# A quarter of an output projection between the steps of the last head pair

## The chip, the cores and the metric

The kernel runs on one core of a Trainium2 chip. The metric is the device time of one execution in microseconds (us); the time of a kernel is the median of its runs. Engines are named as in the profile: PE (TensorE, the matrix engine), PEld (its weight loads), DVE (VectorE), ACT (ScalarE), POOL (GpSimd) and SP (SyncE, which here issues nearly all DMA transfers, in order, on one queue). A name with q (SPq) is an engine's queue.

## The reference

One inference step of a two-layer encoder on 640 frames: 512 of a new stream (the prompt) and 16 each of 8 running streams (the samples). Layer 0 is a convolution module and a gated feed-forward network (FFN); layer 1 is attention over a shared K and V, and an FFN. Cut to the attention:

```python
k, v = jnp.split(rms_norm(h, norm_kv) @ w_kv, 2, axis=-1)
q = (rms_norm(h, norm_attn[j]) @ w_q[j]).reshape(B, T, N_HEADS, HEAD_DIM)
if past_k is None:                                   # the prompt
    o = band_attention_prompt(q, k, v, rel_bias[j])
else:                                                # the samples, with 512 cached rows
    o = band_attention_sample(q, jnp.concatenate([past_k, k], axis=1),
                              jnp.concatenate([past_v, v], axis=1), rel_bias[j])
h = h + o @ w_o[j]
h = h + swiglu(rms_norm(h, norm_ffn[l]) @ w_ffn_in[l]) @ w_ffn_out[l]
```

There are 16 heads of 64 and 1024 features. All data are float32.

## The kernel before

Features lie on the 128 partitions and frames along the free axis, so `h` is 8 feature tiles (KT = 8) of 640 columns (NT), the 128 sample frames first. Each operand of a large matmul is split into a high part (float32r) and a low part, and a product is three matmuls (`mm3`, lines 167 to 169). `wsplit` loads 2048 columns of weights and splits them (ACT the high part, line 147; DVE the low part, line 151), two buffers in turn; `xsplit` splits activations (lines 156 and 157).

The instructions of each engine run in the order in which the compile step puts them: a scheduler with a time model takes them by readiness and by the order in which the program issues them, and a `high_priority` block moves its instructions forward.

The attention goes through 8 head pairs `p` (two heads of 64 fill the 128 partitions). The steps of a pair stand in a string, BO for pairs 0 to 6 and BL for the last:

- `a0`, `a1` (`head_a`): the prompt's scores of one head (lines 1049 and 1050), the maxima with the bias added (DVE, line 959), exponentials (ACT, line 952) and scaling.
- `s0`, `s1` (`samp_a`): scores of four running streams each. Two tiles of cached keys and two of cached values are loaded (line 1100, 512 KB each, tag `cache`, CB = 5 buffers); the scores are lines 1105 and 1108. They go into the PSUM tile that the head of the same number left.
- `b0`, `b1` (`head_b`): transposes of the probabilities (line 1073).
- `t0`, `t1` (`samp_b`): the same for the samples (lines 1121 and 1123).
- `p0` (`pair_c`): probabilities times V for both heads (line 1090), and the split of the result into `oT[p]`.
- `c0`, `c1` (`samp_c`): probabilities times cached V (line 1136) and new V (line 1140), scaling, a transpose (line 1148) and the split.

Between two pairs the next pair's K and Q are projected (`proj_kq`) and, every second pair, V (`proj_v`). After pair 2 `proj_o(0)` adds the output projection of pairs 0 and 1 to `h`, after pair 4 `proj_o(1)` that of pairs 2 and 3. The rest, pairs 4 to 7, follows the loop: for each half of the columns (NH = 320) and each of 8 feature tiles one PSUM tile collects 12 matmuls (4 pairs, three each), and one DVE instruction adds it to `h` (line 1195). `mm` has two PSUM tiles for all of this.

Then the FFN begins. Its first normalisation needs all 8 feature tiles of the first column half: squares (ACT, line 175), sums (POOL or DVE, line 194; PE, line 203), the power (POOL, line 244), the spread over the partitions (PE, line 215), a copy (ACT, line 524), the products (DVE, line 528) and the splits (ACT, line 319; DVE, line 320). Its matmuls are line 383.

Of the kernel before, what the change touches and what calls it, by code (L numbers as in the profile page):

```python
# [12 lines left out]
ALU = mybir.AluOpType  # L13
# [38 lines left out]
NXA, NXB = NB * SEG + HIST + HA, HIST + 320  # L52
SSQ = 'avavavav'
SCUT = 8
CB, QB, KB = 5, 1, 1
NSTD = 3
NH = NT // 2
X11, X21, XT2, XT1, XT3, XT4, X22 = range(7)
# [1 line left out]
HIX = {X11: 0, X21: 1, XT1: 2, XT2: 3, XT3: 4, X22: 5, XT4: 6}  # L60
QORD = "50 a0 10 a1 20 51 11 60 30 21 70 61 31 40 52 71 12 22 41 62 32 53 72 13 23 42 63 33"
BO = "a0 s0 a1 s1 b0 b1 t0 p0 c0 t1 c1"
BL = "a0 s0 a1 s1 t0 b0 b1 c0 t1 c1 p0"
SSQ1 = 'ppapappp'
LNO = ((0, 1, 4, 5, 6, 2, 3, 7), (0, 1, 4, 2, 3, 5, 6, 7))
PLAN = ("a0 y x1 b0 b1 q0 dp1s0 c2 ds1p2 D3 C4 S3 q3 ds2 C5 E6 S4 A4 F6 B4 E7 S5 A5 F7 S6 A6 S7 "
# [8 lines left out]
def tile_trunk(ctx, tc, xT, vecs, hist, w_pw1, w_pw2, w_in0, w_out0, w_os0, w_in1, w_out1, w_os1,  # L75
# [884 lines left out]
                                       op0=ALU.add, op1=ALU.max, accum_out=mx)  # L960

    kts, qts, vts, oT = {}, {}, {}, {}

    def proj_kq(p):
        wh, wl = wsplit(w_kq[p], 16, P, gains=GKQ)
# [57 lines left out]
    def head_a(p, hh):  # L1023
        kt, qt = kts[p], qts[p]
        r = slice(hh * DH, hh * DH + DH)
        S = sp.tile([P, 1280], F32, tag="S", name=nm("S"))
        mx = ap.tile([P, 4], F32, tag="mx", name=nm("mx"), bufs=3)
        sm = ap.tile([P, 4], F32, tag="sm", name=nm("sm"), bufs=3)
        wide = w2t()
        st = w2t()  # L1030
        ro = slice(DH - hh * DH, 2 * DH - hh * DH)
        KK = ap.tile([P, 512], F32R, tag="KK", name=nm("KK"), bufs=KB)
        KL = ap.tile([P, 512], F32R, tag="KL", name=nm("KL"), bufs=KB)
        QQ = ap.tile([P, 512], F32R, tag="QQ", name=nm("QQ"), bufs=KB)
        nc.scalar.activation(out=KK[r], in_=kt[r, P:], func=AF.Copy)
        nc.scalar.activation(out=QQ[r], in_=qt[r, P:], func=AF.Copy)
        nc.gpsimd.tensor_copy(KK[ro], KK[r].bitcast(F32))
        for to in (r, ro):
            nc.vector.tensor_tensor(out=KL[to], in0=kt[r, P:], in1=KK[r].bitcast(F32),
                                    op=ALU.subtract)  # L1040
        nc.vector.tensor_tensor(out=QQ[ro], in0=qt[r, P:], in1=QQ[r].bitcast(F32),
                                op=ALU.subtract)
        pss = []
        for i in ORD:
            n = (i + 1) * P
            o = SOFF[i]
            q = slice(i * P, (i + 1) * P)
            ps = st[:, 640:896] if i == 1 else wide[:, o:o + n]
            nc.tensor.matmul(ps, QQ[:, q], KK[:, 0:n], start=True, stop=False)
            nc.tensor.matmul(ps, QQ[:, q], KL[:, 0:n], start=False, stop=True)  # L1050
            pss.append(ps)
        for ii, i in enumerate(ORD):
            n = (i + 1) * P
            o = SOFF[i]
            addmax(S[:, o:o + n], pss[ii], BP[:, hh, 512 - n:512], mx[:, ii:ii + 1])
        rs = softmax_rows(S, mx, sm, [(SOFF[i], (i + 1) * P) for i in ORD])
        for ii, i in enumerate(ORD):
            n = (i + 1) * P
            o = SOFF[i]
            nc.vector.tensor_scalar(out=S[:, o:o + n], in0=S[:, o:o + n],  # L1060
                                    scalar1=rs[:, ii:ii + 1], scalar2=None, op0=ALU.mult)
        return S, st

    def head_b(S):
        PT = sp.tile([P, 1280], F32, tag="PT", name=nm("PT"))
        for kk in ((0,), (1, 3), (2,)):
            tr = amt()
            base = POFF[kk[0]]
            tot = 0
            for k in kk:  # L1070
                for i in range(k, 4):
                    o = POFF[k] - base + (i - k) * P
                    nc.tensor.transpose(tr[:, o:o + P],  # L1073
                                        S[:, SOFF[i] + k * P:SOFF[i] + (k + 1) * P], ident)
                    tot += P
            if kk[0] == 0:
                nc.scalar.activation(out=PT[:, base:base + tot], in_=tr[:, :tot], func=AF.Copy)
            else:
                nc.vector.tensor_copy(PT[:, base:base + tot], tr[:, :tot])
        return PT  # L1080

    def pair_c(p, PTs):
        VT = vts[p // 2]
        po = amt()
        for k in range(4):
            n = (4 - k) * P
            for hh in range(2):
                r = slice(hh * DH, hh * DH + DH)
                v0 = (p % 2) * P + hh * DH
                nc.tensor.matmul(po[r, k * P:512], VT[:, 1 + k, v0:v0 + DH],  # L1090
                                 PTs[hh][:, POFF[k]:POFF[k] + n], start=(k == 0), stop=(k == 3))
        xsplit(po, oT[p][0][:, P:], oT[p][1][:, P:])

    def samp_a(p, u, st):
        qb, kt = qbd[p % 2], kts[p]
        cache = []
        for src in (kc[p, u], vc[p, u].rearrange("p b k d -> p b (k d)")):
            for i in range(2):
                t = ap.tile([P, 2, 512], F32, tag="cache", name=nm("cache"), bufs=CB)
                nc.sync.dma_start(t, src[:, 2 * i:2 * i + 2, :])  # L1100
                cache.append(t)
        KC, VC = cache[:2], cache[2:]
        qv = [qb[:, 4 * u + b, :, :].rearrange("p h q -> p (h q)") for b in range(4)]
        for b in range(4):
            nc.tensor.matmul(st[32 * b:32 * b + 32, 0:512], qv[b], KC[b // 2][:, b % 2, :],  # L1105
                             start=True, stop=True)
        for b in range(4):
            nc.tensor.matmul(st[32 * b:32 * b + 32, 512:576], qv[b], kt[:, 64 * u:64 * u + 64],
                             start=True, stop=True)
        S = ap.tile([P, 576], F32, tag="Ss", name=nm("Ss"), bufs=2)  # L1110
        mx = ap.tile([P, 4], F32, tag="mx", name=nm("mx"), bufs=3)
        sm = ap.tile([P, 4], F32, tag="sm", name=nm("sm"), bufs=3)
        addmax(S, st[:, 0:576], BS, mx[:, 0:1])
        rs = softmax_rows(S, mx, sm, [(0, 576)])
        return S, rs, VC

    def samp_b(u, S):
        v0 = 64 * u
        tr = amt()
        for k in range(4):  # L1120
            nc.tensor.transpose(tr[:, k * P:(k + 1) * P], S[:, k * P:(k + 1) * P], ident)
        tn = amt()
        nc.tensor.transpose(tn[0:v0 + 64, 0:P], S[:, 512 - v0:576], ident)
        PT = ap.tile([P, 640], F32, tag="PTs", name=nm("PTs"), bufs=1)
        nc.scalar.activation(out=PT[:, 0:512], in_=tr, func=AF.Copy)
        nc.vector.tensor_copy(PT[v0:v0 + 64, 512:640], tn[v0:v0 + 64, 0:P])
        return PT

    def samp_c(p, u, PT, rs, VC):
# [3 lines left out]
        for k in range(5):  # L1133
            for b in range(4):
                if k < 4:
                    nc.tensor.matmul(pv[32 * b:32 * b + 32, 0:P],  # L1136
                                     PT[:, k * P + 32 * b:k * P + 32 * b + 32],
                                     VC[b // 2][:, b % 2, k * P:(k + 1) * P], start=(k == 0), stop=False)
                else:
                    nc.tensor.matmul(pv[32 * b:32 * b + 32, 0:P],  # L1140
                                     PT[v0:v0 + 64, 512 + 32 * b:512 + 32 * b + 32],
                                     VT[v0:v0 + 64, 0, (p % 2) * P:(p % 2) * P + P],
                                     start=False, stop=True)
        os_ = ap.tile([P, P], F32, tag="os", name=nm("os"), bufs=1)
        nc.vector.tensor_scalar(out=os_, in0=pv[:, 0:P], scalar1=rs[:, 0:1], scalar2=None,
                                op0=ALU.mult)
# [3 lines left out]
        for hh in range(2):  # L1150
            r = slice(hh * DH, hh * DH + DH)
            xsplit(trv[r, :, hh, :],
                   oT[p][0][r, v0:v0 + 64].rearrange("p (b q) -> p b q", q=SB),
                   oT[p][1][r, v0:v0 + 64].rearrange("p (b q) -> p b q", q=SB))

    run(proj_kq(0), proj_v(0))
    for p in range(NP):
# [8 lines left out]
        for op in (BL if p == NP - 1 else BO).split():  # L1166
# [5 lines left out]
            elif op[0] == "b":  # L1172
                pt[i] = head_b(ha[i][0])
            elif op[0] == "t":
                ps[i] = samp_b(i, sa[i][0])
            elif op[0] == "c":
                samp_c(p, i, ps[i], *sa[i][1:])
            else:
                pair_c(p, (pt[0], pt[1]))
        if p + 1 < NP:  # L1180
# [3 lines left out]
        if p in PO:  # L1184
            proj_o(PO[p])

    wos = [wsplit(w_o[r], 16, P) for r in (2, 3)]
    for g0, n in ((0, NH), (NH, NH)):
        for m in range(KT):
            pt = mmt()  # L1190
            mm3(pt[:, :n], [(wh[:, (k * 8 + m) * P:(k * 8 + m + 1) * P],
                             wl[:, (k * 8 + m) * P:(k * 8 + m + 1) * P])
                            for wh, wl in wos for k in range(2)],
                [(oT[4 + k][0][:, g0:g0 + n], oT[4 + k][1][:, g0:g0 + n]) for k in range(4)])
            nc.vector.tensor_tensor(out=h[:, m, g0:g0 + n], in0=pt[:, :n], in1=h[:, m, g0:g0 + n],
                                    op=ALU.add)
    at.close()
    early.close()

# [118 lines left out]
```

## Time and profile before

| | |
|---|---|
| time, median of 3 runs | 1525.98 us (1524.56 to 1526.48) |
| the profiled execution | 1530.94 us, span 1528.9 us |
| PE, matmuls | 1456.1 us busy (95%) |
| DVE | 1120.0 us (73%) |
| ACT | 746.7 us (49%) |
| POOL | 281.8 us (18%) |
| DMA | 192.57 MB, 126 GB/s |

Busy times are of the one profiled execution. The span is the time between the first and the last instruction in the trace. A busy PE is not a PE at its peak: matmuls are pipelined, and at a lower granted clock the same matmul is longer. All times of a timeline are microseconds from the span's start. Rows of the view by stretches give start and end, the length, then the busy time of each engine with its instructions in brackets.

### The profile page before, as it was taken

To read this page: it belongs to the slowest core of one execution; us is meant where nothing else is said; L and a number is where in the kernel's file an instruction comes from. 1 tells how busy PE (TensorE), PEld (TensorE's weight loads), DVE (VectorE), ACT (ScalarE), POOL (GpSimd) and SP (SyncE) were. 2 spreads that over 40 slices of the span, in tenths; PEclk is the share of its full clock that TensorE was granted. 3 is DMA by queue.
4 is the path that set the end of the run, shared out by engine and by line. 5 is a ranking of instruction groups with operands and counts; after the bars stand their busy time and mean duration, and the time that the engine had idled before them with its cause. 6 is when DMAs were issued, how large, how long until landed. Compare 5 with 4: busy or idle time off the path is not lost.

```text
span 1528.9 us, 28150 instructions
## 1 busy us (share of the span) xinstructions
PE 1456.1 (95%) x10974; PEld 1378.4 (90%) x10974; DVE 1120.0 (73%) x2481; ACT 746.7 (49%) x1617; POOL 281.8 (18%) x312
## 2 busy tenths in 40 slices
PE   5999899999999999999999999988999999999995
PEld 5998689999999999999887888957999999999994
DVE  5789346798888887856676667653799788688844
ACT  3666245464554563545554454442465464464432
POOL 5789232000000000013221121011000001001001
PEclk9999889999999999999999999988999999999997
DMA  7267414134444444424555455551124543444501
GB/s 236 65 185 182 102 48 132 44 101 117 149 116 126 139 116 132 111 83 149 193 188 189 138 173 187 168 166 42 56 76 111 158 127 93 143 138 92 169 29 69
DMA packets 71013, 192.57 MB, mean 126 GB/s; under 512 B 12000, under 2 KB 33248, under 8 KB 62432
## 3 DMA queue, kind: packets, MB, share of 16 engines
q1 hardware_dynamic: 61664, 175.78, 35.7%
q0 software_dynamic: 8928, 14.68, 6.4%
q8 instruction: 86, 1.41, 0.4%
q10 hardware_dynamic: 288, 0.31, 0.1%
q14 instruction: 47, 0.39, 0.1%
HBM read 179.14 MB, written 11.61 MB: 125 GB/s over the span
## 4 chain that ended last, share of the span: by engine, by line
PE 77%; DVE 8%; POOL 5%; DMA 5%; ACT 3%; issue 2%; SPq 0%; POOLq 0%; DVEq 0%; ACTq 0%
PE mm L383 44%; PE mm L167 7%; PE mm L168 7%; PE mm L169 7%; POOL ca L730 4%; PE mm L768 2%; DMA raw<-in_w_in 1%; PE w L1105 1%; PE w L203 1%; PE am L1090 1%; DVE wlo L320 1%; DMA cache<-in_ck 1%; PE am L1073 1%; PE am L1136 1%; DMA s<-in_w_in 1%
## 5 line engine op out<-in xcount | busy, mean ns | idle before, releaser
L383 PE MATMUL mm<-XH,whi 128*128 128x320 f32 x896 | 275.8, 310 | 4.5 <-DVE t L397 3.0
L383 PE MATMUL mm<-XH,wlo 128*128 128x320 f32 x896 | 276.5, 310 | 0.0
L383 PE MATMUL mm<-XL,whi 128*128 128x320 f32 x896 | 273.8, 309 | 0.0
L319 ACT ACTIVATE whi<-raw 128x512 fp32r<-128x512 f32 (+2 forms) x280 | 166.3, 612 | 156.7 <-PE mm L383 90.5
L167 PE MATMUL mm<-xh,whi 128*128 128x320 f32 (+2 forms) x640 | 202.0, 317 | 4.6 <-ACT xh L156 2.6
L168 PE MATMUL mm<-xh,wlo 128*128 128x320 f32 (+2 forms) x640 | 201.2, 315 | 0.6 <-DVE wlo L151 0.6
L169 PE MATMUL mm<-xl,whi 128*128 128x320 f32 (+2 forms) x640 | 198.1, 314 | 0.0
L320 DVE TENSOR_TENSOR wlo<-raw,whi 128x512 fp32r<-128x512 f32 (+2 forms) x280 | 183.6, 670 | 14.1 <-ACT whi L319 12.7
L383 PE MATMUL mm<-hid,whi 128*128 128x320 f32 x732 | 172.2, 309 | 2.6 <-ACT whi L319 2.3
L383 PEld LDWEIGHTS mm<-XH,whi 128*128 128x128 f32 x896 | 167.8, 188 | 6.5 <-DVE t L397 3.5
L383 PEld LDWEIGHTS mm<-XH,wlo 128*128 128x128 f32 x896 | 168.2, 188 | 0.5 <-DVE wlo L320 0.5
L383 PEld LDWEIGHTS mm<-XL,whi 128*128 128x128 f32 x896 | 167.6, 188 | 0.0
L167 PEld LDWEIGHTS mm<-xh,whi 128*128 128x128 f32 x640 | 122.5, 192 | 8.1 <-ACT xh L156 3.1
L383 PEld LDWEIGHTS mm<-hid,whi 128*128 128x128 f32 x732 | 124.9, 188 | 4.0 <-ACT whi L319 3.4
L365 POOL DMA_DIRECT2D s<-in_w_in x38 | 33.8, 890 | 503.9 <-DVE XL L320 115.7
L168 PEld LDWEIGHTS mm<-xh,wlo 128*128 128x128 f32 x640 | 122.7, 192 | 1.2 <-DVE wlo L151 0.8
L169 PEld LDWEIGHTS mm<-xl,whi 128*128 128x128 f32 x640 | 121.5, 191 | 1.2 <-issue 1.0
L383 PE MATMUL mm<-hid,wlo 128*128 128x320 f32 x366 | 112.5, 308 | 0.0
L383 PE MATMUL mm<-XL,shi 128*128 128x320 f32 x344 | 105.4, 308 | 1.3 <-DVE XL L320 1.3
L383 PE MATMUL mm<-XH,shi 128*128 128x320 f32 x344 | 106.0, 308 | 0.4 <-ACT XH L319 0.4
L383 PE MATMUL mm<-XH,slo 128*128 128x320 f32 x344 | 106.0, 308 | 0.1
L319 ACT ACTIVATE shi<-raw 128x512 fp32r<-128x512 f32 (+1 forms) x114 | 66.4, 587 | 73.5 <-PE mm L383 38.6
(229 smaller groups left out, 3368.7 us busy)
## 6 DMA issues: line engine op xcount, KB each, us to landing
raw<-in_w_in SPq DMA_DIRECT2D x38, 1024.0 KB
raw<-in_w_os SPq DMA_DIRECT2D x24, 768.0 KB
cache<-in_ck SPq DMA_DIRECT2D x32, 512.0 KB
cache<-in_cv SPq DMA_DIRECT2D x32, 512.0 KB
raw<-in_w_pw SPq DMA_DIRECT2D x12, 1024.0 KB
s<-in_w_in SPq DMA_DIRECT2D x38, 256.0 KB
s<-in_w_in POOLq DMA_DIRECT2D x38, 256.0 KB, 4.8
raw<-in_w_kq SPq DMA_DIRECT2D x8, 1024.0 KB
```

Of the source, the lines that this page charges most:

```text
L167: nc.tensor.matmul(ps, wh, xh, start=(i == 0), stop=False)
L168: nc.tensor.matmul(ps, wl, xh, start=False, stop=False)
L169: nc.tensor.matmul(ps, wh, xl, start=False, stop=(i == last))
L203: nc.tensor.matmul(st[:, 512 + t * w + k:513 + t * w + k], s[:, a:a + P], onec, start=True, stop=True)
L319: nc.scalar.activation(out=hi, in_=src, func=AF.Copy)
L320: nc.vector.tensor_tensor(out=lo, in0=src, in1=hi.bitcast(F32), op=sub)
L365: nc.gpsimd.dma_start(s1, src[:, 3 * n:4 * n], accum_op=add)
L383: nc.tensor.matmul(pt, wt, v, start=(first and k == i == 0), stop=(k == len(xs) - 1 and i == 2), skip_group_check=True)
L730: nc.gpsimd.tensor_tensor(out=acc, in0=acc, in1=pr, op=ALU.add)
L768: nc.tensor.matmul(pt[32 * q:32 * q + 32, 0:n], w4[0:r, 4 * tg + q, :], mv, start=(tg == 0), stop=(tg == 7))
L1073: nc.tensor.transpose(tr[:, o:o + P], S[:, SOFF[i] + k * P:SOFF[i] + (k + 1) * P], ident)
L1090: nc.tensor.matmul(po[r, k * P:512], VT[:, 1 + k, v0:v0 + DH], PTs[hh][:, POFF[k]:POFF[k] + n], start=(k == 0), stop=(k == 3))
```

## The change

The output projection of pairs 4 and 5 (weights `w_o[2]`, a quarter of the whole) is taken out of the part after the loop. It becomes a generator, `halves(2)`, that does one PSUM tile of 6 matmuls and its addition to `h` at a time and stops after every second tile, so in eight portions of 12 matmuls. The token `o2`, set eight times into BL, runs one portion. Each portion is traced inside `tc.issue_after(step_end[0])`, which keeps its PE instructions behind the last PE instruction of the step before. The order of the other steps is as it was. Pairs 6 and 7 follow the loop as `halves(3)`, 6 matmuls to a PSUM tile. There are as many matmuls as before, but 32 additions to `h` in place of 16. The cache tag gets eight buffers for five.

```diff
-CB, QB, KB = 5, 1, 1
+CB, QB, KB = 8, 1, 1
...
-BL = "a0 s0 a1 s1 t0 b0 b1 c0 t1 c1 p0"
+BL = "a0 s0 o2 a1 o2 s1 o2 t0 o2 b0 b1 o2 c0 t1 o2 c1 o2 p0 o2"
...
+    fill, step_end = None, [None]
...
-            nc.tensor.matmul(ps, QQ[:, q], KL[:, 0:n], start=False, stop=True)
+            step_end[0] = nc.tensor.matmul(ps, QQ[:, q], KL[:, 0:n], start=False, stop=True).ins
...
+    def halves(r):
+        wh, wl = wsplit(w_o[r], 16, P)
+        for g0 in (0, NH):
+            for m in range(KT):
+                pt = mmt()
+                mm3(pt[:, :NH], [(wh[:, (k * 8 + m) * P:(k * 8 + m + 1) * P],
+                                  wl[:, (k * 8 + m) * P:(k * 8 + m + 1) * P]) for k in range(2)],
+                    [(oT[2 * r + k][0][:, g0:g0 + NH], oT[2 * r + k][1][:, g0:g0 + NH])
+                     for k in range(2)])
+                nc.vector.tensor_tensor(out=h[:, m, g0:g0 + NH], in0=pt[:, :NH],
+                                        in1=h[:, m, g0:g0 + NH], op=ALU.add)
+                if m % 2:
+                    yield
...
+            elif op[0] == "o":
+                if fill is None:
+                    fill = halves(i)
+                with tc.issue_after(step_end[0]):
+                    next(fill)
...
-    wos = [wsplit(w_o[r], 16, P) for r in (2, 3)]
-    for g0, n in ((0, NH), (NH, NH)):
-        for m in range(KT):
-            pt = mmt()
-            mm3(pt[:, :n], [(wh[:, (k * 8 + m) * P:(k * 8 + m + 1) * P],
-                             wl[:, (k * 8 + m) * P:(k * 8 + m + 1) * P])
-                            for wh, wl in wos for k in range(2)],
-                [(oT[4 + k][0][:, g0:g0 + n], oT[4 + k][1][:, g0:g0 + n]) for k in range(4)])
-            nc.vector.tensor_tensor(out=h[:, m, g0:g0 + n], in0=pt[:, :n], in1=h[:, m, g0:g0 + n],
-                                    op=ALU.add)
+    next(fill, None)
+    for _ in halves(3):
+        pass
```

The other steps set `step_end[0]` in the same way to their last PE instruction.

More of the change, by code (lines that the diff above doesn't have):

```diff
@@ L1072, in head_b @@
                     o = POFF[k] - base + (i - k) * P
-                    nc.tensor.transpose(tr[:, o:o + P],
-                                        S[:, SOFF[i] + k * P:SOFF[i] + (k + 1) * P], ident)
+                    step_end[0] = nc.tensor.transpose(
+                        tr[:, o:o + P], S[:, SOFF[i] + k * P:SOFF[i] + (k + 1) * P], ident).ins
                     tot += P
@@ L1089, in pair_c @@
                 v0 = (p % 2) * P + hh * DH
-                nc.tensor.matmul(po[r, k * P:512], VT[:, 1 + k, v0:v0 + DH],
-                                 PTs[hh][:, POFF[k]:POFF[k] + n], start=(k == 0), stop=(k == 3))
+                step_end[0] = nc.tensor.matmul(
+                    po[r, k * P:512], VT[:, 1 + k, v0:v0 + DH],
+                    PTs[hh][:, POFF[k]:POFF[k] + n], start=(k == 0), stop=(k == 3)).ins
         xsplit(po, oT[p][0][:, P:], oT[p][1][:, P:])
@@ L1107, in samp_a @@
         for b in range(4):
-            nc.tensor.matmul(st[32 * b:32 * b + 32, 512:576], qv[b], kt[:, 64 * u:64 * u + 64],
-                             start=True, stop=True)
+            step_end[0] = nc.tensor.matmul(st[32 * b:32 * b + 32, 512:576], qv[b],
+                                           kt[:, 64 * u:64 * u + 64], start=True, stop=True).ins
         S = ap.tile([P, 576], F32, tag="Ss", name=nm("Ss"), bufs=2)
@@ L1122, in samp_b @@
         tn = amt()
-        nc.tensor.transpose(tn[0:v0 + 64, 0:P], S[:, 512 - v0:576], ident)
+        step_end[0] = nc.tensor.transpose(tn[0:v0 + 64, 0:P], S[:, 512 - v0:576], ident).ins
         PT = ap.tile([P, 640], F32, tag="PTs", name=nm("PTs"), bufs=1)
@@ L1139, in samp_c @@
                 else:
[L1140 to L1143, printed above, removed]
+                    step_end[0] = nc.tensor.matmul(
+                        pv[32 * b:32 * b + 32, 0:P],
+                        PT[v0:v0 + 64, 512 + 32 * b:512 + 32 * b + 32],
+                        VT[v0:v0 + 64, 0, (p % 2) * P:(p % 2) * P + P], start=False, stop=True).ins
         os_ = ap.tile([P, P], F32, tag="os", name=nm("os"), bufs=1)
```

## The prediction

> **What bounds the kernel now.** I read the page first, then tables by stage, then the timeline of each engine around the attention's end.
>
> ```profile
> span 1528.9 us, 28150 instructions
> ...
> PEclk9999889999999999999999999988999999999997
> ...
> 729.00:1000.00 271.00, 268.52 (x2327) 231.57 (x2326) 181.87 (x544) 131.78 (x358) 50.70 (x90) 1.00 0.53 175
> ...
> 1007.40:1047.10 39.70, 27.93 (x234) 16.79 (x230) 18.32 (x63) 14.73 (x40) 1.56 (x2) 0.79 0.41 132
> 1047.10:1061.00 13.90, 13.58 (x83) 12.99 (x83) 4.51 (x10) 3.23 (x7) 5.26 (x6) 0.88 0.38 95
> 1061.00:1081.00 20.00, 18.03 (x130) 17.68 (x129) 11.65 (x26) 6.31 (x13) 0.88 (x1) 1.00 0.00 1
> 1081.00:1528.80 447.80, 424.42 (x2864) 420.68 (x2864) 350.03 (x723) 214.61 (x450) 30.93 (x35) 0.98 0.38 108
> ```
>
> The first row gives the span, the second the granted TensorE clock in 40 slices. The others are stretches, with the busy time of PE, PE's weight loads, DVE, ACT and POOL, then clock, DMA share and GB/s. Head pairs 0 to 6 and their projections (729 to 1000) keep PE busy for 268.52 of 271 us: 2.5 us is all that can be won there. The last pair is different: nothing is left to project beside it, so from 1007.4 to 1047.1, which I call the zone, PE works 27.93 of 39.70 us at a clock of 0.79. The tail of the output projection follows, its first column half to 1061, its second to 1081, where the FFN starts. The profiled execution took 1530.94 us, 2.0 more than its span and 4.96 more than the median of 1525.98; I make the sum on this execution and carry the difference to the median.
>
> Two views say what the zone loses: PE's waits in it (us in total, times, longest), and finer stretches.
>
> ```profile
> PE w L1105 <- DMA cache<-in_ck: 4.3, 2, 2.2
> PE mm L167 <- ACT ohi L156: 4.0, 2, 3.0
> PE w L1105 <- DVE mx L959: 1.1, 1, 1.1
> ...
> 1010.40:1013.80 3.40, 1.05 (x4) 0.14 (x4) 2.37 (x7) 1.33 (x5) 0.00 (x0) 0.90 0.81 298
> 1013.80:1020.00 6.20, 6.16 (x49) 4.16 (x53) 3.10 (x14) 2.41 (x9) 0.00 (x0) 0.50 0.46 149
> 1020.00:1023.40 3.40, 2.39 (x29) 0.92 (x21) 1.85 (x10) 2.16 (x8) 0.00 (x0) 1.00 0.48 130
> 1023.40:1026.90 3.50, 1.39 (x13) 0.50 (x13) 1.25 (x6) 1.06 (x6) 0.00 (x0) 0.99 1.00 383
> 1026.90:1030.20 3.30, 3.29 (x14) 3.13 (x15) 1.63 (x8) 1.45 (x3) 0.95 (x1) 0.50 0.11 25
> ...
> 1033.60:1037.00 3.40, 2.01 (x35) 1.18 (x31) 1.01 (x4) 1.03 (x3) 0.00 (x0) 1.00 0.00 0
> 1037.00:1043.80 6.80, 6.33 (x51) 2.83 (x44) 0.80 (x3) 0.43 (x2) 0.00 (x0) 0.50 0.01 2
> ```
>
> PE is idle for 39.7 - 27.93 = 11.8 us: 4.3 for the sample group's cached keys, 4.0 for the split attention output (3.0 of it at the very end), the rest in short waits for DVE and ACT. And it works at half clock for 6.16 + 3.29 + 6.33 = 15.8 us, which at full clock would be 7.9. So the zone holds 27.93 - 7.9 = 20.0 us of PE work.
>
> **The change, part by part.** The tail first: its matmuls, their pitch, and what stands on the other engines. The first two rows are groups (busy, mean ns), the others instructions with their start, duration and, in brackets, the idle time before them.
>
> ```profile
> L167 PE MATMUL mm<-ohi,whi 128*128 128x320 f32 x4 | 1.3, 329 | 0.0
> ...
> L167 PE MATMUL mm<-ohi,whi 128*128 128x320 f32 x58 | 19.0, 328 | 4.9 <-ACT ohi L156 3.0 <-DVE h L1195 1.9
> ...
> 1047.37 0.47 PE L168 MATMUL mm<-ohi,wlo 128*128 128x320 f32 x1
> 1047.64 0.47 PE L167 MATMUL mm<-ohi,whi 128*128 128x320 f32 x1
> ...
> 1050.95 0.30 PE L167 MATMUL mm<-ohi,whi 128*128 128x320 f32 x1
> 1060.47 0.31 PE L169 MATMUL mm<-olo,whi 128*128 128x320 f32 x1
> ...
> 1081.03 0.41 PE L383 MATMUL mm<-XH,shi 128*128 128x320 f32 x1 [0.41 <-ACT XH L319]
> ...
> L1195 DVE TENSOR_TENSOR h<-mm,h x16: 482/492/493, 1048.8 to 1079.4; 128x320 f32<-128x320 f32 x16
> ...
> 980.73 1.91 ACT L147 ACTIVATE whi<-raw 128x2048 fp32r<-128x2048 f32 x1 [2.83 <-PE mm L168]
> ```
>
> Each of the three lines 167 to 169 issues 64 of these matmuls, 192 in all. Per line 4 ran between 1000.5 and 1002.7 (the x4 group) and 58 after 1047 (the x58 group), so 174 stand in the tail and 18 before it. Between the rows at 1050.95 and 1060.47 lie 65 steps: 9.52 / 65 = 0.1465 us a matmul at full clock. The two rows at 1047 show 0.27 at half clock.
>
> After the change 96 matmuls, those of head pairs 4 and 5, stand in the zone in eight portions of 12 (1.76 us each), and 96, those of pairs 6 and 7, in the tail. The first column half of the tail is then 48 matmuls: 48 x 0.1465 = 7.0 us, beginning warm, in place of 13.9: **-6.9**. The 6 of pair 6 that already run in the zone may do so again; I count them in the tail, the dearer place.
>
> The second half loses 48 matmuls, 7.0 us of PE, so PE has 18.03 - 7.0 = 11.0 us to do there. DVE's 11.65 us stay, since 16 sums still fall into the tail; and the FFN's first normalisation now has half as many matmuls to hide it:
>
> ```profile
> 1060.82 0.49 DVE L1195 TENSOR_TENSOR h<-mm,h 128x320 f32<-128x320 f32 x1 [1.27 <-PE mm L169]
> ...
> 1061.40 0.47 ACT L175 ACTIVATE sq<-h 128x320 f32<-128x320 f32 x1 [1.28 <-DVE h L1195]
> ...
> 1064.45 0.72 PE L203 MATMUL w<-onec,sq 128*128 128x1 f32 x6
> 1065.66 0.88 POOL L244 TENSOR_TENSOR rst<-rst,mhalf 128x3 f32<-128x3 f32 x1 [6.28 <-DVE rst L237]
> 1067.90 0.83 PE L215 MATMUL w<-ident,rst 128*128 128x128 f32 x6
> 1069.07 0.42 ACT L524 ACTIVATE hid<-w 128x320 f32<-128x320 f32 x1
> 1069.60 3.79 DVE L528 SCALAR_TENSOR_TENSOR hid<-h,vec,hid 128x320 f32<-128x320 f32 x8
> ...
> 1078.62 1.99 ACT L319 ACTIVATE whi<-raw 128x1024 fp32r<-128x1024 f32 x2
> 1080.52 2.98 ACT L319 ACTIVATE XH<-hid 128x320 fp32r<-128x320 f32 x8
> ```
>
> From the last sum of the first half to the first split tile the bare chain is 0.47 + 0.72 + 0.88 + 0.83 + 0.42, one eighth of 3.79 and one of 2.98: 4.2 us, well inside 11.0. What took 19.7 us before (1061.31 to 1081.03) was queueing, at the end behind the weight split of 1078.62, whose buffers the output projection held. One of these buffers now comes free before the tail. But PE and DVE are nearly even, so they will not pack perfectly: the best is DVE's 11.65 (-8.4), the worst the old 20.0 (the first rival). I take 11.0 plus 3 us of waiting, nearer the best because the chain is short: 14.0 for 20.0, **-6.0**.
>
> The zone gets 96 x 0.1465 = 14.1 us of PE work on top of its 20.0: 34.1 us if the clock stays up and nothing waits, 5.6 less than 39.7. The waits for cached keys should go: with eight buffers a whole pair's keys and values have their own, and the first load no longer waits for the previous pair's last sample step. Of the final 3.0 the last portion hides 1.8; of the some 3.5 us of short waits I let half stay. That leaves about 2.9 us: 34.1 + 2.9 - 39.7 = **-3** (rounded). The other end is from DVE: 16 more sums at 0.49 us make 7.9 us, and each waits for its portion on DVE's queue ahead of the next step's maxima and scalings. If all of it fell on the chain of the last pair, the zone would be 4.9 longer than now. DVE is busy for 18.32 of 39.7 us there, so I stay near the other end.
>
> Edits costed at nothing: the 12 matmuls that leave 1000.5 to 1002.7 (PE then waits for the pair's own steps; at most their 1.8 us come back as a gain). The weights of the moved quarter, loaded and split early already (980.73, some 27 us ahead of their first portion). The instruction handles kept in a variable. In pairs 0 to 6 the eight buffers can win at most the 2.5 us of PE's idle time; I take 0, and the loss is a rival. The FFN after its start keeps its 447.8 us.
>
> The sum: -6.9 - 6.0 - 3 = -15.9, so 1515.0 for this execution, **1510.1** for the median.
>
> **A rule weighed: the clock.** In the rows above half clock follows not a silent stretch but a thin one: after 1.05 of 3.4 us busy, after 1.39 of 3.5, and after 2.01 of 3.4, while 2.39 of 3.4 kept it. So a stretch of 3.4 us must be about two thirds busy; the zone's average would be 34.1 of 37.0. One thin stretch left over would cost about 1.7 us, which lies inside the bounds. [...]
>
> **The rivals.**
>
> ```profile
> 1007.11 6.68 DMA cache<-in_ck
> ...
> SPq L1100 <- PE am L1136: 52.5, 14, 9.0
> ```
>
> *The normalisation becomes the bound of the tail.* The second half keeps its 20 us, since the statistics, DVE's 11.65 us and the splits keep their queue order. Then the sum is -6.9 - 3 = -9.9, or 1516.1; with the zone at its bad end (+4.9) it is 1524. For it speaks that DVE is already the fuller engine, against it the 4.2 us of the bare chain. I give it 0.23, most of it near 1516 and up to 1521.
>
> *The portions stand in front of the pair's steps* and nothing of them is hidden: a step that is ready when a portion has just begun waits 1.76 us for it, the last pair's chain grows by as much, its thin stretches stay and the clock with them. At 0.265 us a matmul the zone grows by 96 x 0.265 = 25.4 us and the tail gives back 12.9: +12.5, **slower, 1538.5**. It decides from the point where the zone grows by more than 12.9 us, so with nothing hidden even at full clock (14.1). Against it speak the 11.8 us of idle PE. 0.06.
>
> *The loads queue badly in pairs 0 to 6.* All loads stand on SP's one queue, where cache loads waited for buffers for 52.5 us behind the value products alone. With eight buffers more of them go ahead of the next projection's weights. Two cache loads took 6.68 us from issue to landing, one 3.3; if each of the seven projections' weights came later by that and PE stood for it, that is +23.4, and with -15.9 the result is +7.5, 1533.5. It turns the sign from 2.3 us a pair. Against it: PE stands for no more than 2.5 us in these 271 now. 0.06.
>
> *The change does little*, because the order made at compile time puts the portions where PE has work anyway: 1526, 0.05.
>
> **How the numbers follow.** The forecast has 0.60, and its own range is 1505 (both good ends: -6.9 - 8.4 - 5.6 = -20.9) to 1517 (the zone 4 longer, not 3 shorter). The range over the cases goes down by the further 2.5 us of pairs 0 to 6 to 1503, and up to 1521, where the first rival meets a zone that grows by 2. A measurement of this kernel tells about 0.2%, 3 us, from no change. Faster is the forecast and the first rival, 0.83; within 0.2% is 0.05; slower the other two, 0.12.
>
> **What would show it.** In the profile after: 96 matmuls of lines like 167 to 169 between the last pair's steps; a granted clock of 1.00 in nearly all of the zone, no wait of L1105 for cached keys, and a zone of 34 to 39 us; a tail from the last split output to the first FFN matmul of about 21 us instead of 33.9. A tail of 27 us with PE waiting for XH is the first rival. A zone of more than 52 us, a clock of 0.5 in the portions, or PE idle time of well over 2.5 us in pairs 0 to 6 would make the forecast wrong.

## The result and the profile after

The change made the kernel faster: 1516.63 us (1515.33 to 1517.9) against 1525.69 in the first comparison, ratio 0.9938 [0.9923, 0.9952]. Two later comparisons of the same kernel gave 1511.47 against 1523.97 and 1511.52 against 1524.84, both 0.9919 [0.9898, 0.994]. So it saves 9 to 13 us; forecast were 15.9. The profiled execution took 1517.9 us, 13.0 less than the one of before.

From the page of the kernel after:

```profile
span 1516.1 us, 28173 instructions
...
PEclk9999899999999999999999999999899999999997
```

The table by stretches of the kernel after (start and end, length, busy time of PE, weight loads, DVE, ACT and POOL, then clock, DMA share, GB/s). The first row is pairs 0 to 6 from their first scores, the second the zone, the next two the tail, the last the FFN:

```profile
726.06:1001.18 275.12, 272.49 (x2436) 239.16 (x2434) 190.03 (x564) 138.76 (x369) 54.53 (x91) 1.00 0.53 176
1001.25:1037.70 36.45, 32.72 (x322) 25.69 (x322) 24.80 (x78) 14.59 (x41) 1.57 (x2) 1.00 0.33 109
1037.70:1053.00 15.30, 11.69 (x57) 10.90 (x58) 8.72 (x16) 5.47 (x10) 5.22 (x6) 0.78 0.51 154
1053.00:1068.90 15.90, 12.55 (x75) 12.29 (x74) 11.52 (x28) 6.38 (x17) 0.89 (x1) 0.78 0.00 2
1068.90:1516.00 447.10, 424.92 (x2865) 421.99 (x2864) 346.33 (x716) 211.58 (x444) 30.92 (x35) 0.97 0.37 105
```

PE's largest waits from 1001 to 1069 in the kernel after (total, times, longest):

```profile
PE mm L167 <- DVE h L1167: 6.4, 3, 3.3
PE am L1125 <- ACT PTs L1127: 1.3, 2, 0.7
PE w L1107 <- DVE mx L959: 1.1, 1, 1.1
```

The zone is as forecast: 36.5 us at a clock of 1.00, PE busy for 32.72, no wait for cached keys. The tail is not: 31.1 us in place of 33.9, at a clock of 0.78, with 6.4 us of waiting for the sums on DVE. And pairs 0 to 6, for which I had put nothing, are 8 to 9 us shorter. The stretches of every profile, in the same marks (pairs: from the first scores of pair 0 to the first of the last pair; zone: to the first output matmul that reads `oT[7]`; tail: to the first FFN matmul, F). "Cold" is 20 us times one minus the granted clock of the first 20 us after F; S is the start of the 22nd SiLU of that FFN (the expectations call it the 23rd, since the load of its table stands first on that line), a mark that every kernel reaches with the same work done. F and S are counted from the first scores of pair 0.

| kernel | median us | pairs 0-6 | zone | tail | F | cold | S | S - F - cold |
|---|---|---|---|---|---|---|---|---|
| before | 1525.69 | 283.8 | 39.7 | 33.9 | 357.4 | 0.0 | 541.4 | 184.0 |
| before2 | 1524.84 | 283.2 | 36.7 | 35.3 | 355.2 | 0.0 | 539.2 | 184.0 |
| por5 | 1523.02 | 281.8 | 42.8 | 28.9 | 353.5 | 0.0 | 537.0 | 183.5 |
| cb8 | 1512.17 | 276.5 | 30.2 | 35.8 | 342.5 | 0.0 | 526.6 | 184.1 |
| keys5 | 1514.48 | 276.6 | 30.8 | 35.8 | 343.1 | 0.0 | 527.2 | 184.1 |
| after | 1516.63 | 275.1 | 36.5 | 31.1 | 342.7 | 1.8 | 528.1 | 183.6 |
| after2 | 1511.47 | 275.1 | 36.5 | 31.1 | 342.7 | 1.8 | 527.9 | 183.4 |
| after3 | 1511.52 | 275.1 | 36.5 | 31.4 | 343.1 | 0.0 | 526.6 | 183.5 |
| sev | 1509.56 | 275.1 | 36.5 | 27.5 | 339.2 | 0.0 | 522.8 | 183.6 |
| sev2 | 1510.89 | 275.1 | 36.5 | 27.6 | 339.2 | 0.0 | 522.8 | 183.6 |
| behind1 | 1512.18 | 275.2 | 36.5 | 24.8 | 336.5 | 2.8 | 523.0 | 183.7 |
| am4 | 1512.54 | 275.1 | 36.5 | 23.2 | 334.8 | 7.6 | 526.6 | 184.2 |
| unpin | 1511.71 | 277.9 | 35.7 | 26.3 | 339.9 | 3.0 | 526.3 | 183.4 |
| unpinsev | 1512.67 | 277.9 | 38.7 | 26.9 | 343.5 | 1.8 | 528.7 | 183.4 |

The last column lies between 183.4 and 184.2 in all fourteen: from F to S every kernel takes the same time once the cold start is taken off, so what a kernel gains up to F it keeps, less what PE then loses at half clock. What lies outside these marks, before pair 0 and behind S, takes between 979.6 us (unpinsev) and 988.2 (behind1), and 982.4 to 988.0 for one and the same kernel (after2, after). In one kernel that is chance, and it is larger than the differences among the versions with medians from 1509.6 to 1514.5; the marks tell them apart, the medians do not.

### The profile page after: what moved, and what is told of

Same layout as the page of the kernel before. It is cut to its first block, busy times and chain, and to the rows that moved or that the text cites. A ratio compares the mean times of both kernels' runs of the same rounds, so it can differ in the third digit from the quotient of the medians.

```text
span 1516.1 us, 28173 instructions
## 1 busy us (share of the span) xinstructions
PE 1444.0 (95%) x10974; PEld 1376.8 (91%) x10974; DVE 1124.5 (74%) x2497; ACT 745.3 (49%) x1617; POOL 285.7 (19%) x312
## 4 chain that ended last, share of the span: by engine, by line
PE 75%; DVE 9%; DMA 5%; POOL 5%; ACT 4%; issue 2%; SPq 0%; POOLq 0%; DVEq 0%; ACTq 0%
PE mm L383 44%; PE mm L167 7%; PE mm L168 7%; PE mm L169 7%; POOL ca L730 4%; DMA raw<-in_w_in 2%; PE mm L768 2%; DVE wlo L320 2%; PE w L203 2%; DMA s<-in_w_in 1%; PE am L1091 1%; PE w L1107 1%; PE am L1074 1%; ACT whi L139 1%; PE am L1138 1%
## 5 line engine op out<-in xcount | busy, mean ns | idle before, releaser
L383 PE MATMUL mm<-XH,wlo 128*128 128x320 f32 x896 | 276.5, 309 | 0.0
L320 DVE TENSOR_TENSOR wlo<-raw,whi 128x512 fp32r<-128x512 f32 (+2 forms) x280 | 183.3, 669 | 12.9 <-ACT whi L319 11.6
L319 ACT ACTIVATE shi<-raw 128x512 fp32r<-128x512 f32 (+1 forms) x114 | 66.3, 587 | 73.6 <-PE mm L383 42.8
```

What stands on the lines that cost most here:

```text
L319: nc.scalar.activation(out=hi, in_=src, func=AF.Copy)
L320: nc.vector.tensor_tensor(out=lo, in0=src, in1=hi.bitcast(F32), op=sub)
L383: nc.tensor.matmul(pt, wt, v, start=(first and k == i == 0), stop=(k == len(xs) - 1 and i == 2), skip_group_check=True)
```

## The experiments

**Which part does it? The buffers alone (cb8), the portions alone (por5), and before again (before2).** In cb8 the kernel before gets one edit, in por5 the kernel after gets the opposite one:

```diff
-CB, QB, KB = 5, 1, 1      # cb8, in the kernel before
+CB, QB, KB = 8, 1, 1
...
-CB, QB, KB = 8, 1, 1      # por5, in the kernel after
+CB, QB, KB = 5, 1, 1
```

> The kernel before, profiled a second time. In the first pair of profiles the stretch from the first scores of pair 0 (723.6) to the end of the last K and Q projection (1000.5) took 276.9 us before and 269.6 after (726.1 to 995.7). If that was the chance of one execution, this profile shows about 270 and an execution near the median of 1525.7. If the eight buffers won it, it shows about 277 again.

> Eight cache buffers alone, no portions. Theory A (the buffers give a large part of the gain): pairs 0 to 6 take about 270 us instead of 277, the two waits for cached keys in the last pair (4.3 us) go, the tail stays at 33.9: 5 to 8 us faster than before, about 1519. Rival B (the difference in pairs 0 to 6 is chance): only the 4.3 us count, and part of them turns into other waits of the last pair: 1 to 4 us faster, about 1523.

> The eight portions alone, with five cache buffers. Theory A: the tail gets shorter by 2 to 3 us as in the full change, the last pair keeps its waits for cached keys but the portions stand in them: 2 to 4 us faster than before, about 1523. Rival B (the portions give most of the gain): 6 to 9 us faster, about 1518.

Measured: before2 0.9998 [0.9977, 1.002]; cb8 1512.17 us, 0.9915 [0.9891, 0.9939]; por5 1523.02 us, 0.9984 [0.9964, 1.0003]. Pairs 0 to 6 took 283.2 us again in before2, so the 8 us are not a chance of one profile. The buffers alone bring the whole gain, 12 us and more than either theory gave; the portions alone bring 1.5 us, which the noise does not tell from nothing (by the interval at most 5.5). Two stages show where. First PE's groups for the sample scores in pairs 0 to 6, of before2, cb8 and after (busy us, mean ns):

```profile
L1105 PE MATMUL w<-cache,qbd 128*32 128x512 f32 x112 | 22.3, 605 | 0.0
L1108 PE MATMUL w<-kt,qbd 128*32 128x64 f32 x112 | 6.6, 222 | 0.0
```

```profile
L1105 PE MATMUL w<-cache,qbd 128*32 128x512 f32 x112 | 17.0, 605 | 0.0
L1108 PE MATMUL w<-kt,qbd 128*32 128x64 f32 x112 | 5.0, 220 | 0.0
```

```profile
L1107 PE MATMUL w<-cache,qbd 128*32 128x512 f32 x112 | 17.0, 605 | 0.0
L1110 PE MATMUL w<-kt,qbd 128*32 128x64 f32 x112 | 5.0, 220 | 0.0
```

As many instructions with the same mean, and yet 22.3 + 6.6 - 17.0 - 5.0 = 6.9 us less busy time: they overlap more. PE's timeline shows how, first one sample step of before2, then one of cb8:

```profile
793.60 1.05 PE L1105 MATMUL w<-cache,qbd 128*32 128x512 f32 x4
...
800.68 0.62 PE L1105 MATMUL w<-cache,qbd 128*32 128x512 f32 x2
801.13 0.60 PE L1105 MATMUL w<-cache,qbd 128*32 128x512 f32 x2
```

```profile
768.74 1.07 PE L1105 MATMUL w<-cache,qbd 128*32 128x512 f32 x8
```

A step has eight rows, for four streams whose 32 columns of scores lie side by side. Issued together, all eight are through in 1.07 us. Issued in two parts, since the second tile of keys has its place in the order later, half of them takes as long, and the step 1.05 + 1.05. Of the 14 steps in pairs 0 to 6, 7 are split so in before2 and por5, 2 in cb8 and in after. Five fewer, at 1.05 us, make 5.3 us, which is the difference of L1105 (22.3 - 17.0). The 6.9 us fit the 6.7 by which pairs 0 to 6 are shorter in cb8 (283.2 to 276.5). So the matmuls of the four streams run beside each other when they are issued together (eight rows of 605 ns on average in 1.07 us), and issued two and two they take twice as long.

Then the zone and the tail, of before2 (the zone only, with PE's key scores in it), cb8 (the zone with the same group, then the tail and PE's longest wait at its start) and por5:

```profile
1006.72:1043.39 36.67, 25.44 (x234) 14.25 (x230) 18.29 (x63) 14.74 (x40) 1.57 (x2) 0.86 0.43 143
...
L1105 PE MATMUL w<-cache,qbd 128*32 128x512 f32 x16 | 5.1, 717 | 4.5 <-DMA cache<-in_ck 3.1 <-DVE mx L959 1.1 <-DVE rs L955 0.3
```

```profile
996.64:1026.84 30.20, 20.42 (x234) 13.89 (x230) 18.21 (x63) 14.53 (x40) 1.57 (x2) 0.94 0.40 122
...
L1105 PE MATMUL w<-cache,qbd 128*32 128x512 f32 x16 | 2.1, 605 | 1.7 <-DVE mx L959 1.7
...
1026.84:1062.67 35.83, 33.30 (x210) 32.29 (x210) 16.19 (x35) 9.56 (x20) 6.13 (x7) 0.90 0.15 38
...
PE mm L167 <- ACT ohi L156: 3.0, 1, 3.0
```

```profile
1003.35:1046.16 42.81, 37.53 (x327) 28.22 (x323) 24.93 (x78) 14.79 (x41) 1.57 (x2) 0.92 0.42 129
1046.16:1075.01 28.85, 21.45 (x130) 20.31 (x130) 18.69 (x39) 9.77 (x21) 6.12 (x7) 0.88 0.28 83
```

The buffers alone take the zone from 36.7 (39.7 in the first profile) to 30.2 at a clock of 0.94. They do it less by closing holes than by shortening what PE does: of before2's 11.2 us of idle PE (36.67 - 25.44) the 3.1 for cached keys go, but other waits grow, and 9.8 are left in cb8 (30.20 - 20.42), the 3.0 for the last split output among them. PE's busy time falls by 5.0 us, 3.0 of it at L1105 (both steps of the last pair were split before), and the clock is higher (0.94 against 0.86). The portions do fill holes: with them PE stands for 3.7 us of the zone. But 6.3 us of them lengthen it (30.2 to 36.5), and the tail gives back only 4.8 (35.8 to 31.1). Pairs 0 to 6 are 1.4 shorter, and that is no saving: 12 output matmuls (1.76 us) run before the last pair's first scores in before and cb8, none in after and por5. Up to F that makes 342.5 us without the portions and 342.7 with them: nothing.

**Is it the number of buffers, or that a step's keys come as one? (keys5)** The memory of before, five times 512 KB: the keys of a step in one tile of 1 MB with one transfer, its values in the three buffers that are left.

```diff
+        KC = ap.tile([P, 4, 512], F32, tag="keys", name=nm("keys"), bufs=1)
+        nc.sync.dma_start(KC, kc[p, u])
...
+            t = ap.tile([P, 2, 512], F32, tag="cache", name=nm("cache"), bufs=3)
...
-            nc.tensor.matmul(st[32 * b:32 * b + 32, 0:512], qv[b], KC[b // 2][:, b % 2, :],
+            nc.tensor.matmul(st[32 * b:32 * b + 32, 0:512], qv[b], KC[:, b, :],
```

> The kernel before, in the same memory: the four running streams' keys of a sample step in one tile of 1 MB (one buffer), the values in three tiles of 512 KB, in place of five tiles for both. The four key matmuls of a step then become ready together. In the order of the kernel before, 7 of the 14 sample steps of pairs 0 to 6 have them in two groups with other work between; with eight buffers 2; here 1. Theory A (pairs 0 to 6 gained 7 us with eight buffers because matmuls on different column strips of PE run side by side only when they stand together): lines 1105 and 1108 fall from 22.3 and 6.6 us of PE time in pairs 0 to 6 to about 17 and 5, and pairs 0 to 6 from 283 to about 276 us, with no earlier load. Rival B (the earlier loads won it): pairs 0 to 6 stay at 283 us or grow, as a single key buffer loads later. The last pair may wait longer for its keys than the 4.3 us of before.

Measured: 1514.48 us, 0.9936 [0.9914, 0.9959]. The groups of pairs 0 to 6 and the zone of keys5:

```profile
L1105 PE MATMUL w<-keys,qbd 128*32 128x512 f32 x112 | 16.0, 605 | 0.6 <-DMA keys<-in_ck 0.6
L1108 PE MATMUL w<-kt,qbd 128*32 128x64 f32 x112 | 4.4, 219 | 0.0
```

```profile
998.97:1029.72 30.75, 20.62 (x233) 12.69 (x229) 18.19 (x63) 14.64 (x40) 1.56 (x2) 1.00 0.51 171
```

One step is split instead of seven, which at 1.05 us is 6.3, as measured (22.3 - 16.0). Pairs 0 to 6 take 276.6 us and the zone 30.8, as with eight buffers. So the gain needs no more memory and no portions. In pairs 0 to 6 it comes from the four matmuls of a step finding their keys together, and not from the whole step being loaded earlier. For the fourth and the eighth step the transfer of the keys is issued 6.9 and 10.0 us ahead of the scores in keys5, and 12.0 and 12.4 in cb8; in before2 it was 6.5 and 6.7 for the first tile and 0.2 for the second. In the zone one of the two steps is still split (L1105 takes 3.1 us there); what else shortens it is a clock of 1.00 and a wait of 1.1 us for keys in place of 3.1.

**Where did the portions' gain in the tail go? (behind1, sev, sev2, am4)** In the kernel after DVE's timeline and PE's (start, duration, in brackets the idle time before and what ended it), and one row of the chain that ended last:

```profile
1039.43 2.36 DVE L320 TENSOR_TENSOR wlo<-raw,whi 128x1024 fp32r<-128x1024 f32 x2
1041.70 0.89 DVE L1167 TENSOR_TENSOR h<-mm,h 128x320 f32<-128x320 f32 x2
...
1048.54 0.69 DVE L369 TENSOR_TENSOR raw<-raw 128x512 f32<-128x512 f32 x1 [2.19 <-DMA raw<-in_w_in]
1049.15 0.88 DVE L1167 TENSOR_TENSOR h<-mm,h 128x320 f32<-128x320 f32 x2
...
1051.75 0.49 DVE L1167 TENSOR_TENSOR h<-mm,h 128x320 f32<-128x320 f32 x1 [0.39 <-PE mm L169]
...
1058.77 3.78 DVE L528 SCALAR_TENSOR_TENSOR hid<-h,vec,hid 128x320 f32<-128x320 f32 x8
1062.47 0.88 DVE L1167 TENSOR_TENSOR h<-mm,h 128x320 f32<-128x320 f32 x2
```

```profile
1042.25 0.63 PE L167 MATMUL mm<-ohi,whi 128*128 128x320 f32 x1 [2.11 <-DVE h L1167]
...
1049.69 0.41 PE L167 MATMUL mm<-ohi,whi 128*128 128x320 f32 x1 [0.92 <-DVE h L1167]
...
1063.01 0.64 PE L167 MATMUL mm<-ohi,whi 128*128 128x320 f32 x1 [3.35 <-DVE h L1167]
```

```profile
1041.82 6.62 DMA raw<-in_w_in
```

`mm` has two PSUM tiles, and with 6 matmuls to a tile instead of 12 a sum is due every 0.9 us (6 x 0.1465). In the order of DVE's instructions three others stand ahead of sums: the split of the first FFN weights (1039.43), a step of the next weights (1048.54) that waits 2.19 us for a transfer of 6.62, and the normalisation's eight products (1058.77). No sum passed them: that of the six matmuls that end at 1047.41 (the last starts at 1046.94 and takes 0.47) starts at 1049.15, behind the step that waits. PE stands for 2.11, 0.92 and 3.35 us, 6.4 in all, and its clock halves at the first and the last: the granted clock is 0.50 from 1041.5 and from 1062.0, and a matmul of 320 columns is issued every 0.27 us (1042.68 to 1043.74) in place of 0.15 (1050.08 to 1050.66). In the kernel before, a tile took 12 matmuls, so that a sum was due every 1.8 us (12 x 0.1465), and the buffer for those weights came free late: the transfer that starts at 1041.82 here started at 1082.21 there, behind the whole tail, and the split of 1039.43 stood at 1079.83, behind the last sum.

behind1 puts nearly all of the FFN's early weight work on DVE behind the last sum, sev only the step that waits for the transfer; am4 gives the tail four PSUM tiles:

```diff
...
+            with tc.issue_after(tail_add[0]) if tail_add[0] is not None else nullcontext():   # sev
+                ws = w_seven_(src, out)
+            tail_add[0] = None
...
-                pt = mmt()                                                                    # am4
+                pt = amt() if r == 3 and m % 2 else mmt()
```

(`tail_add[0]` is the last sum of the tail; behind1 puts the same context around the other weight splits of that time as well.)

> The full change, and DVE's work for the FFN's weights 1 to 3 is kept behind the last sum of the output projection. Theory A (the expected gain of the tail went to DVE, where two weight splits of 2.36 us and a step waiting 2.2 us for its load stand ahead of the sums, PE idles and loses its clock): the tail falls from 31.2 us to about 25, PE's waits for sums from 6.4 to about 3.5, the time to about 1510.5. Rival B (the normalisation sets the tail's end whatever DVE does): the tail stays within 1.5 us of 31, the time at 1516. Rival C: the weights now come too late for the FFN, PE waits for them after its start, and the time stays at 1516 with a short tail.

> The full change again, beside the others. So far the eight buffers alone took 1512.2 us and the full change 1516.6, not side by side. From the first scores of the last pair to the first FFN matmul the profiles show 66.0 us with the buffers alone (30.2 in the last pair, 35.8 in the tail) and 67.8 with the portions too (36.5 and 31.2). Theory A (the portions cost the pair what they take from the tail): this run stays 1 to 5 us slower than 1512.2, with the stretch again at 67 to 69 us. Rival B (the difference is chance between sessions): 1512 to 1513.

> The full change, and only DVE's steps for the first seven-product weights, which wait for a load, are kept behind the last sum of the output projection; the two weight splits of 2.36 us stay ahead of the sums. Theory A (the wait for the load costs the tail PE time and clock): the tail falls from 31.2 by 2 to 4 us, PE's wait of 0.9 us at that place goes, the FFN loses nothing, as these weights are first used some 60 us after its start. Rival B (the splits ahead of the sums are what costs): the tail falls by less than 1 us.

> The full change with four PSUM tiles for the sums of the tail in place of two (the two tiles of the pairs' steps are free there). Theory A (the tail is long because PE may run only two tiles ahead of DVE, whose queue holds weight work and the normalisation): PE's waits for sums fall from 6.4 us to under 3, the clock stays up, the tail falls to 26 to 28 us. Rival B (DVE itself is the bound of the tail, 20.2 us of work and the waits for loads in 31.2): PE's waits fall but the FFN starts within 1.5 us of the same time.

> The full change with that one edit again, beside the full change itself: 3 to 5 us faster than it, about 1507.5, and again 522 to 524 us to the 23rd SiLU. If the first run's 5 us were chance, it is within 1 us of the full change.

Measured: behind1 1512.18 us, 0.9915 [0.989, 0.994]; after2 0.9919, as told above; sev 1509.56, 0.992 [0.9892, 0.9949]; am4 1512.54, 0.9934 [0.9909, 0.9959]; sev2 1510.89, 0.991 [0.9885, 0.9934]. after2 repeats the stretches of after to 0.1 us, and its median is no slower than cb8's. All three edits shorten the tail, to 24.8, 27.5 and 23.2 us, so DVE's order and the two PSUM tiles are what held it. PE's waits for sums, 6.4 us in the kernel after, are 3.8 in behind1, 5.5 in sev and 1.7 in am4; in sev, whose tail is 3.5 us shorter, a part of the gain is clock (0.88 in the tail of sev2, 0.78 in that of after). But the times hardly move. PE's wait in am4, then stretches of am4 around F (1055.77), then the first 20 us behind F in am4, after2 and sev2:

```profile
PE mm L383 <- ACT XH L319: 4.2, 1, 4.2
```

```profile
1052.37:1055.77 3.40, 0.00 (x0) 0.00 (x0) 3.40 (x6) 2.56 (x7) 0.00 (x0) 0.70 0.15 24
1055.77:1059.17 3.40, 3.40 (x13) 3.37 (x14) 3.40 (x8) 3.40 (x8) 0.00 (x0) 0.50 0.72 287
...
1065.97:1069.37 3.40, 3.40 (x14) 3.40 (x14) 1.31 (x9) 0.00 (x0) 0.00 (x0) 0.50 0.00 0
1069.37:1072.77 3.40, 3.40 (x22) 3.40 (x22) 0.00 (x0) 0.44 (x1) 0.00 (x0) 0.79 0.00 0
...
1055.77:1075.77 20.00, 20.00 (x95) 19.96 (x96) 11.44 (x35) 7.67 (x16) 0.00 (x0) 0.62 0.13 50
```

```profile
1064.08:1084.08 20.00, 20.00 (x129) 20.00 (x130) 9.65 (x28) 7.56 (x14) 0.00 (x0) 0.91 0.16 53
```

```profile
1031.78:1059.37 27.59, 21.55 (x130) 20.77 (x130) 18.70 (x39) 10.89 (x24) 6.11 (x7) 0.88 0.30 86
1059.37:1079.37 20.00, 20.00 (x141) 20.00 (x141) 12.90 (x36) 10.11 (x20) 0.00 (x0) 1.00 0.15 53
```

am4 reaches F first of all, but only after 4.24 us without a matmul, and starts the FFN at half clock: 95 matmuls in 20 us, against 129 and 141. That is 20 x (1 - 0.62) = 7.6 us, and its lead of 7.9 over after2 is 1.3 at S. behind1 loses 2.8 so, sev and sev2 nothing: they keep their 3.5 us, and are 3.8 to 5.3 us ahead of after, after2 and after3 at S, twice the same (522.8). The medians, 1.9 and 0.6 us below the kernel after of their own comparisons, don't resolve it. sev is the best version that I found, by its marks; that it beats cb8 or the change is not shown by times. sev's edit without the portions was not run, so what the portions are worth beside it stays open.

**Does the place of the matmuls matter? (unpin, unpinsev)** With eight buffers kept, the portions are not tied to the steps: both quarters follow the loop, and the compile step may move them forward. unpinsev adds sev's edit.

```diff
-BL = "a0 s0 o2 a1 o2 s1 o2 t0 o2 b0 b1 o2 c0 t1 o2 c1 o2 p0 o2"
+BL = "a0 s0 a1 s1 t0 b0 b1 c0 t1 c1 p0"
...
-    next(fill, None)
-    for _ in halves(3):
-        pass
+    for r in (2, 3):
+        for _ in halves(r):
+            pass
```

> Eight buffers, and the projection of pairs 4 and 5 by itself after the loop, as its own sums, but not pinned between steps: the compile step may place it. In the order that it makes, all 16 sums of this quarter stand before the last pair's output is split, most of them beside the end of pair 6 and the last pair's first steps. Theory A (the portions cost the pair because they are pinned in front of ready steps): the last pair takes 31 to 34 us with the same matmuls in it, the tail 29 to 32, the time is 2 to 4 us below the full change. Rival B (14.1 us of matmuls lengthen the last pair wherever they stand, since with eight buffers it has few holes): the last pair takes 36 us or more, the time is that of the full change.

> The unpinned quarter with eight buffers, and DVE's steps for the first seven-product weights behind the last sum. Theory (the wait for that load costs the tail some 2 to 3 us wherever the quarter stands): from the first scores of pair 0 to the 23rd SiLU of the FFN 522 to 524 us in place of 526.3, as the pinned kernel fell from 528 to 522.8 by the same edit. If the unpinned order has no such wait on its path, it stays at 526.

> The full change once more, as the reference beside the two kernels above: 1511 to 1513, 528 us to the 23rd SiLU.

The zone and the tail of unpin:

```profile
997.31:1033.03 35.72, 29.24 (x305) 22.97 (x301) 25.66 (x76) 16.66 (x42) 1.57 (x2) 1.00 0.35 111
1033.03:1059.37 26.34, 21.59 (x126) 20.54 (x127) 17.45 (x39) 9.61 (x24) 6.13 (x7) 0.86 0.24 61
```

unpin took 1511.71 us, 0.9929 [0.9902, 0.9956]: the compile step fills the zone by itself (35.7 us, as with the pinned portions, though 24 output matmuls already run before it; so nearer to rival B), F comes 2.8 us sooner than in after2, and 3.0 are lost at a cold start. unpinsev, 1512.67 us, 0.9926 [0.99, 0.9953], went against my theory: its tail of 26.9 us is no shorter than unpin's, its zone 3.0 longer, its S 2.4 later. In this order the edit of sev is no gain; why its zone got longer was not followed up. after3 repeats after2 in the median and up to F (343.1 against 342.7).

## Why the prediction was right, and where it was not

The direction and the range were right: 1516.63 and 1511.5 lie in 1503 to 1521. The sum up to F was -15.9, measured -14.7 against the first profile of before and -12.5 against the second. But two of its terms were wrong by nearly the same amount in opposite directions, so that the sum came out near is luck; and the portions, the idea of the change, bring nothing that the buffers do not bring alone (342.7 us up to F against 342.5).

*Pairs 0 to 6: bounded at -2.5, taken as 0, measured -8 (283.2 in before2 to 275.1, 6.7 of it in cb8).* The failed step is "In pairs 0 to 6 the eight buffers can win at most the 2.5 us of PE's idle time". Idle time bounds only what waiting costs. Here 6.9 us of busy time was itself a product of late keys. The other 1.4 are the 12 output matmuls that left this stretch, which the prediction named with at most 1.8 and put at nothing. The trace of before shows the splits: rows of L1105 with x4 that take 1.05 us, beside rows with x8 that take 1.07. I had quoted the waits of L1105 only for the last pair.

*The zone: -3, measured -3.2 (39.7 to 36.5), but -0.2 against before2 (36.7).* Clock, waits and length came out as written, the composition did not. I had the portions fill the 11.8 us of idle PE and warm the clock. cb8 shows that the buffers alone do -9.5 (-6.5 against before2), and the portions then cost 6.3 for 14.1 us of matmuls: a little over half is hidden, in the 9.8 us of idle PE that the buffers leave.

*The tail: -12.9, measured -2.8 (-4.2 against before2).* The first half was to take 7.0 us; from 1037.71 to the eighth sum (1051.75) it took 14.0, no less than before (13.7 by the same marks): two waits for sums, and half clock behind the first. The second half was to take 14.0 and took 17.0 (20.2 before): the 3.35 us behind the products and half clock to the end. The failed step is the same in both. I counted DVE's busy time, in which 16 sums stayed 16, but not its order; and I named the freed weight buffer as a gain, when what it lets start early stands ahead of the sums. So what the first rival said of DVE's queue happened, though not at XH: PE waited for the sums. The first median lay on the rival's figure of 1516.1, but not by its terms, since it too had nothing for pairs 0 to 6.

*The FFN "keeps its 447.8 us"*: 447.1, with 1.8 us of cold start hidden in it. The other two rivals did not happen: PE's idle time in pairs 0 to 6 is 2.63 us, and the portions are half hidden. The 3.3 us for one cache load in the rival on the loads was half of the row of 6.68, an estimate; that row is one load of keys, issued at 1007.11.

*The clock rule.* Half clock again followed thin stretches: in the kernel after, the waits of 2.11 and 3.35 us. But the two thirds do not hold. The kernel before has a thinner stretch than the 2.01 us that lost the clock, and it kept it:

```profile
1071.20:1074.60 3.40, 1.81 (x13) 1.55 (x12) 3.20 (x8) 0.72 (x2) 0.00 (x0) 1.00 0.00 0
```

So which thin stretches cost the clock stays open; PE's busy share alone does not decide it. Half clock (0.50) lasts 3.4 or 6.8 us at a time in the zone and tail of before, and in the kernel after 6.8 us (1041.5 to 1048.3) and 10.2 (1062.0 to 1072.2, past F). The first of these two began in a wait of 2.11 us, and PE's longest wait in the zone and the tail there was 3.35.

## What to carry to other kernels

Idle time of the busiest engine does not bound a gain (in pairs 0 to 6 2.5 us of it, and 6.7 won). Look also for one group of its instructions whose rows of different count have the same length (x4 in 1.05 us and x8 in 1.07 here): there busy time can depend on which instructions are issued together. When work is moved off the end of a stage, read the in-order queue of the engine that frees its tiles, instruction by instruction: what starts early there takes the place of what was removed (6.4 us of waits for sums here). And where a stage ends in a wait, count the matmuls of the next 20 us: a lead gained in front of a cold start is given back behind it (in am4 7.9 us at F, 1.3 at S).

## What I had not expected of the hardware

Four matmuls with 32 columns each (eight rows of the trace) take 1.07 us together (cb8 at 768.74), and two of them 1.05 (before2 at 793.60).

The clock took long to return in one case: in am4 it stayed at 0.50 from 1055.77 until 1070.8, some 15 us, in which PE is busy in every row of am4 above. Among the matmuls there stand three groups of six with a single moving column, the last one at 1063.84; whether these kept the clock down was not tried. The clock came back 15 us after the first matmul of the FFN and 5.7 after the end of that last group.
